# Weight gradient on one core: whole rows of G for slice 0, single transfers for slices 4 and 5, a shorter warm-up, five plain pairs at the front, and a new order of work

## The chip, the core and the metric

The kernel runs on one core of one Trainium2 chip. The metric is the device time of one execution in microseconds. Three runs of the kernel before gave 161.97, 161.98 and 162.1; their median is 161.98.

## What is computed

```python
def setup_inputs():
    batch, m, k, n = 16, 512, 1024, 768
    return {
        "input": np.random.randn(batch, m, k).astype(np.float32),
        "grad_output": np.random.randn(batch, m, n).astype(np.float32),
    }

def reference(input, grad_output):
    grad_weight = np.einsum('bmk,bmn->kn', input, grad_output)
    return grad_weight.astype(np.float32)
```

With batch and m joined, X (`input`) has 8192 rows of 1024 columns and G (`grad_output`) has 8192 rows of 768. The output is X transposed times G, 1024 x 768, a sum over the 8192 rows.

## The kernel before

**Tiling.** The rows are cut into 64 slices of 128 rows. TensorE contracts over the 128 rows of a slice: 128 columns of X are the stationary operand and 384 columns of G (its left or right half) the moving one. This document calls one such product, 128 x 128 by 128 x 384 in bf16, a *block*. The output takes 8 x 2 = 16 blocks of each slice.

**Pairs.** Slices 2u and 2u+1 form pair u. The string `LOADS` says how each of the 32 pairs is treated. An `s` pair is *plain*: 32 blocks, nothing else. A `P` pair is *merged*: it is multiplied by a scheme of the Strassen-Winograd kind, seven products of 4 blocks (q = 0 to 3), so 28 blocks, and VectorE first makes the combined operands, three steps for X (`x0`, `x1`, `x2`: lines 199, 201, 203) and three for G (`g0`, `g1`, `g2`: lines 209, 211, 213). Step `x2` writes the X block that stream B of that pair uses. Before, pairs 0 to 3 and 31 are plain and 4 to 30 are merged: 5 x 32 + 27 x 28 = 916 blocks.

**Loads.** Everything but the first transfers goes through GpSimd's DMA queue, which converts float32 to bf16 on the way (lines 170, 171, 175, 177). A pair with u >= `MERGED` comes as one transfer of G and one of X for its 256 rows (two rows for each partition). A pair with u < `MERGED` comes slice by slice. Slice 0 of G and slices 0 and 1 of X come as float32 through SyncE's and ScalarE's queues (lines 145 to 148) and are rounded to bf16 by VectorE and ScalarE (`round_by`, line 217). The kernel loads G of slice 0 in two halves of 384 columns. All other transfers stand in GpSimd's queue in the order of the pairs: G, then X.

**Warm-up.** Before the first data, line 153 runs the matmuls of `WARMUP` on constants: `("b", 512)` is a bf16 matmul of 512 columns, `("f", 512)` a float32 one, which the profile shows as two records.

**The order of the work** is written out by hand in `PLAN`, a list of tokens that is walked once; each engine executes its own part strictly in that order. The tokens:

- `C0@7.1` opens the sum of stream C, block q = 0, in PSUM bank 7 and multiplies one block; `C0.2` multiplies two more. Streams A, B, C, D are the four quarters of the output (A and B the upper half of the rows of the output, C and D the lower; A and C the left half of the columns). Streams 1, 5, 6, 7 are further products of the merged pairs. Stream A (`PACKED`) keeps its sums in banks 0 to 2 throughout.
- `c` and `v` close a sum: ScalarE copies it out (`c`, line 363), or VectorE adds it to the sum in SBUF (`v`, line 367; lines 355, 356 and 360 at the very end; line 365 when it is the first). `f` (line 295) lets ScalarE copy a sum back into a bank. `z` (line 379) puts a bank aside and `y` (line 388) adds it later on VectorE. `w` (line 395) lets GpSimd add one sum in SBUF to another.
- `x1.5`, `g0.5` are the VectorE steps of pair 5 above. `r0` to `r4` are the roundings in `ROUNDINGS`.

The last tokens before end with `... vD3 B0.2 D0.2 vB0 B3.4 vD0 B3.2 cB3`; each finished quarter block is stored at once (line 342), through SyncE's queue except the larger piece of the last one.

`SPARE_LOADS` issues the weight load once more ahead of every second matmul in a range (line 323).

Of the kernel before, what the change touches and what calls it, by code (L numbers as in the profile page):

```python
# [9 lines left out]
P = 128  # L10

LOADS = "ssssPPPPPPPPPPPPPPPPPPPPPPPPPPPs"
# [3 lines left out]
    "A0.1 A2.1 C0@7.1 A3.1 C2@6.1 cC0 r0 C3@3.1 C1@4.1 cC2 A1.1 vC3 B1@5.1 cC1 B2@7.1 D3@6.1 r1 D0@3.1 r4 r2 "  # L16
    "D1@4.1 cB1 D1.1 A0.1 B2.1 cD1 D0.1 B0@5.1 cD3 A3.1 vD0 A2.1 r3 A1.1 B3@6.1 vB0 cB2 B3.1 D3@4.1 B0@3.1 "
    "D2@7.1 vD3 D2.2 B0.1 vB3 B1@5.1 cD2 B1.1 A3.1 C3@4.1 vB1 C3.1 C2@6.2 vC3 A2.1 B3@7.1 C1@5.3 B3.1 B0.1 "
    "vC1 A1.2 C2.1 vB3 B1@4.1 D1@5.1 zcC2.20 D1.1 vB1 B2@7.2 A0.1 vB0 A0.1 A2.1 vD1 D3@6.2 D0@4.1 vB2 D0.1 "
    "A3.1 C3@5.1 vD0 D2@3.1 C0@7.2 vD3 C0.2 vD2 C0.1 C3.2 B3@6.2 vC3 B1@3.2 A3.1 vC0 D3@5.2 vB1 A1.2 B2@4.1 "  # L20
    "vD3 B2.1 D2@3.1 A0.1 yC2.20 A0.1 A3.1 D0@7.1 vB2 D0.1 A2.2 vD2 B0@5.2 D1@4.1 vD0 D1.3 vB0 C0@7.2 A3.1 "
    "vD1 A3.1 A1.1 vC0 B3.1 D2@5.3 fC1@7 B3.1 D0@4.1 vD2 D0.1 A0.2 vD0 fD3@5 C1.3 vB3 C1.1 A2.2 g0.4 cC1 "
    "C3@4.1 B2@6.1 fC2@3 B2.1 g1.4 D3.2 fB0@7 vB2 C3.1 C2.1 cD3 C2.1 g2.4 C2.1 x0.4 C2.2 A2.1 12@5.1 cC2 C3.1 "
    "x1.4 A1.2 c12 x2.4 11@6.1 C0@3.1 fC1@5 vC3 B0.3 c11 vC0 A3.1 C1.1 A0.1 B3@6.1 cC1 61@3.1 B1@4.1 vB3 cB0 "
    "B1.2 c61 73@5.1 g0.5 71@6.1 10@7.1 vB1 13@3.1 x0.5 13.1 A1.1 12@4.1 c13 10.1 A3.1 v12 71.1 c10 73.1 "
    "50@3.1 x1.5 c71 50.1 11@4.1 g1.5 51@7.1 c50 51.1 v11 60@6.1 c73 60.1 61@3.1 g0.6 c51 A2.1 53@5.1 v61 "
    "53.1 fC0@4 A0.1 63@7.1 c53 g2.5 63.1 52@3.1 g1.6 52.1 70@5.1 g2.6 70.1 c52 C0.1 x0.6 C0.1 A1.1 A3.1 cC0 "
    "72@3.1 x2.5 72.2 x1.6 70.1 73@4.1 A0.1 c70 x2.6 63.1 60.1 v73 A2.1 c63 B0@5.2 g0.7 c72 B2@4.2 c60 B2.1 "
    "vB0 62@7.1 fC1@3 62.1 g1.7 62.1 B3@6.1 vB2 B3.1 c62 C1.2 g2.7 C2@4.1 fC0@7 vB3 C2.2 f13@5 C1.1 x0.7 A2.1 "
    "A0.1 cC1 C0.1 11@6.1 vC2 11.1 f51@3 A1.1 13.1 v11 13.1 51.2 x1.7 c13 A3.1 53@6.1 cC0 x2.7 53.1 52@4.1 "  # L30
    "c51 52.1 v53 71@5.2 f50@7 C3@3.1 g0.8 C3.1 f12@6 C3.1 50.1 g1.8 50.1 12.1 g2.8 12.2 x0.8 A2.1 C3.1 c12 "
    "A1.1 A3.1 vC3 52.1 71.1 50.1 x1.8 zc52.20 73@6.2 v71 fB1@3 A0.1 61@4.2 x2.8 c50 61.1 72@5.1 v73 72.1 "
    "fB2@7 B1.2 v72 f10@6 B1.2 B2.1 v61 B2.1 cB1 63@5.1 g0.9 63.1 f51@4 10.3 fC2@3 x0.9 10.1 A1.1 cB2 A3.1 "
    "A2.1 g1.9 51.1 zc63.5 x1.9 51.1 62@7.1 c10 g2.9 62.2 x2.9 c51 A0.1 C2.1 v62 fB3@5 C2.1 60@6.2 y63.5 60.1 "
    "fB0@7 B3.2 v60 cC2 B3.1 11@4.2 y52.20 cB3 B0.2 f13@3 g0.10 B0.1 53@6.2 cB0 13.1 x0.10 13.2 f70@7 A3.1 "
    "11.1 g1.10 c13 A1.1 53.1 x1.10 70.1 f52@5 70.1 v11 70.2 A0.1 g2.10 fB2@4 52.1 x2.10 52.1 C1@3.1 c70 v53 "
    "C1.2 c52 B2.1 C3@7.1 vC1 C3.1 f72@5 B2.1 C0@6.1 vC3 C0.1 cB2 C0.1 72.1 g0.11 f73@3 B1@7.2 A2.1 c72 x0.11 "
    "A2.1 A1.1 f71@4 73.2 vC0 73.1 f63@5 71.1 g1.11 71.1 c73 71.1 x1.11 A0.1 72@6.1 c71 g2.11 72.1 63.1 x2.11 "
    "63.1 fB0@4 63.1 v72 61@3.2 c63 61.1 g0.12 B0.1 fC2@6 B0.1 60@5.1 v61 60.1 cB0 A3.1 g1.12 C2.2 v60 12@3.2 "
    "cC2 12.1 x0.12 12.1 fC3@4 B1.1 A1.1 A2.1 f53@5 g2.12 A3.1 vB1 C3.1 f51@6 C3.1 53.1 v12 53.1 cC3 50@7.2 "  # L40
    "x1.12 50.1 fC1@4 50.1 g0.13 A0.1 c53 51.2 x2.12 51.1 C1.1 g1.13 B3@5.1 c51 B3.1 v50 B3.1 f13@3 C1.1 "
    "52@6.1 vB3 52.1 cC1 13.2 x0.13 13.1 f62@4 11@5.2 c13 11.1 x1.13 A0.1 62.1 v52 62.1 f70@3 62.2 g2.13 "
    "61@7.2 c62 x2.13 70.2 v61 fC0@6 70.1 B2@4.2 v11 c70 B2.1 C0.2 vB2 f71@3 C0.1 A3.1 f73@7 10@5.1 g0.14 "
    "10.3 B1@4.1 x0.14 A2.2 zcB1.4 71.2 10.1 x1.14 f51@4 71.1 73.1 g1.14 73.1 c71 x2.14 73.1 51.1 g2.14 51.1 "
    "c73 A1.2 v10 c51 A0.1 B3@7.1 g0.15 cC0 B3.1 A3.1 63@3.1 vB3 fB1@6 63.2 B0@5.1 g1.15 f70@4 B0.1 v63 B0.1 "
    "B1.2 g2.15 72@7.2 cB1 vB0 72.1 70.1 C2@3.1 x0.15 f52@5 C2.3 53@6.2 vC2 53.1 70.1 52.1 v53 52.2 72.1 "
    "x1.15 f11@6 C1@3.2 v72 C1.1 c52 A2.1 A0.1 vC1 c70 13@7.2 60@5.1 yB1.4 f10@3 60.2 g0.16 60.1 11.2 x0.16 "
    "11.1 10.2 c11 13.1 v60 A1.2 f62@4 A3.1 x1.16 A3.1 f71@6 A2.1 v13 50@5.3 g1.16 50.1 f12@7 g0.17 62.2 "
    "zc50.18 62.1 12.1 g1.17 12.1 c62 12.1 g2.16 12.1 x2.16 71.1 fB1@4 71.1 g2.17 C3@5.1 c12 C3.1 x2.15 C3.2 "
    "x0.17 C3.1 10.1 A2.1 C0@7.1 c10 vC3 C0.2 c71 C0.1 x1.17 A3.1 A0.1 fB2@6 x2.17 A0.1 B0@3.1 g0.18 B0.2 "  # L50
    "B2.1 vC0 B2.3 vB0 B1.3 g1.18 C2@7.2 cB1 g2.18 73@5.2 cB2 vC2 73.1 C1@3.1 f61@4 C1.1 x0.18 C1.1 A1.1 "
    "zc73.3 51@6.2 vC1 51.2 C2@5.1 x1.18 fB3@3 61.2 vC2 61.3 x2.18 f53@5 63@7.2 g0.19 63.1 c61 63.1 53.2 v63 "
    "f52@4 53.1 B3.2 g1.19 f12@7 B3.1 v51 B3.1 A0.1 c53 52.1 12.1 cB3 12.1 13@5.1 x0.19 f71@6 13.2 12.1 "
    "72@3.1 x1.19 72.2 v13 72.1 71.2 v12 71.1 70@5.2 g0.20 70.1 f60@7 70.1 52.1 v72 52.2 60.1 g1.20 60.1 c52 "
    "x2.19 60.2 c71 A1.1 v70 A1.1 11@3.1 f10@6 g2.19 11.2 x0.20 11.1 fB3@5 10.3 v11 A3.2 c10 A3.1 x1.20 A2.1 "
    "fB1@3 73@4.1 x2.20 73.2 g0.21 B3.1 60.1 62@6.1 v73 62.1 c60 62.2 g2.20 B1.1 C0@4.1 g1.21 C0.1 cB1 y50.18 "
    "C0.1 C2@7.1 cB3 C2.1 g2.21 B1@3.2 v62 fB2@5 A2.3 x0.21 B2.3 vC0 C2.1 71@6.2 zcC2.1 vB1 A0.1 51@4.1 cB2 "
    "51.1 g0.22 51.1 A0.1 f72@5 50@7.1 v71 50.3 g1.22 50.1 C1@3.2 v50 C1.1 72.2 x1.21 C3@7.2 g2.22 c72 C3.1 "
    "v51 C3.2 C1.1 x0.22 A1.3 zcC1.10 12@6.1 f63@5 12.1 x1.22 12.1 53@4.1 f13@3 53.1 v12 53.2 63.1 x2.21 63.2 "
    "x2.22 63.1 B0@6.1 g0.23 B0.1 c63 B0.2 v53 B0.1 A0.1 vC3 A0.1 f70@4 13.3 f52@5 x0.23 13.1 70.2 c13 70.1 "  # L60
    "g1.23 A3.1 fC0@7 x1.23 A3.1 52.1 vB0 52.3 g2.23 61@3.2 g0.24 61.3 70.1 C0.1 v61 C0.1 c70 C0.1 62@6.1 "
    "y73.3 c52 62.2 cC0 x2.23 B3@4.3 g1.24 f71@5 B3.1 v62 A3.2 A0.1 x0.24 A0.1 A2.3 vB3 71.3 x1.24 73@4.2 "
    "yC1.10 c71 73.2 fB2@7 50@6.1 g2.24 50.1 v73 11@5.3 x2.24 B2.1 f60@4 B2.1 v11 B2.1 f62@3 B2.1 60.1 g0.25 "
# [12 lines left out]
    "C1.1 A2.2 f73@3 A1.3 vC1 fB1@6 wD2 D1.2 x2.30 73.2 cD1 x2.29 B1.2 vA3 B1.1 fB2@7 B1.2 v73 fD2@4 B1.2 "
    "C2.1 vA2 C2.1 f53@3 C2.2 vA1 C2.1 53.2 cC2 53.1 vB1 53.1 B2.1 fC3@5 B2.1 v53 B2.1 fD3@2 B2.3 f50@6 C3.1 "
    "vA0 C3.2 wB3 50.1 vB2 50.3 vC3 D2.1 fB0@7 D2.1 D3.1 v50 D3.1 cD2 B0.2 fD0@5 B0.3 fB3@3+4 vD3 B0.2 D0.2 "
    "vB0 B3.4 vD0 B3.2 cB3 "
# [8 lines left out]
MERGED = 2  # L88
# [364 lines left out]
```

## Time and profile before

| what | us |
|---|---|
| median of three runs | 161.98 |
| profiled execution, its own time | 161.87 |
| its span (first to last instruction) | 160.1 |
| outside the span | 1.77 |
| TensorE busy in the span | 154.8 |
| VectorE busy | 145.1 |
| ScalarE busy | 99.3 |
| first matmul on data | 5.04 |
| end of the last matmul | 156.7 |

TensorE is busy for 97% of the span. Between the first and the last matmul on data it stands still only in a few short places; the view of instructions in order of time shows them as an idle time in square brackets, with what ended it. The view of stages gives the busy time of each engine for a stretch of the span. In that view the columns are the stretch, its length, and for each engine the busy time with the number of instructions.

### The profile page before, as it was taken

To read this page: it belongs to the slowest core of one execution; us is meant where nothing else is said; L and a number is where in the kernel's file an instruction comes from. 1 tells how busy PE (TensorE), PEld (TensorE's weight loads), DVE (VectorE), ACT (ScalarE), POOL (GpSimd) and SP (SyncE) were. 2 spreads that over 40 slices of the span, in tenths; PEclk is the share of its full clock that TensorE was granted. 3 is DMA by queue.
4 is the path that set the end of the run, shared out by engine and by line. 5 is a ranking of instruction groups with operands and counts; after the bars stand their busy time and mean duration, and the time that the engine had idled before them with its cause. 6 is when DMAs were issued, how large, how long until landed. Compare 5 with 4: busy or idle time off the path is not lost.

```text
span 160.1 us, 2989 instructions
## 1 busy us (share of the span) xinstructions
PE 154.8 (97%) x1002; PEld 98.9 (62%) x1129; DVE 145.1 (91%) x335; ACT 99.3 (62%) x227; POOL 39.1 (24%) x73
## 2 busy tenths in 40 slices
PE   8999999999999999999999999999999999999891
PEld 3466666567677777776656566666666566666461
DVE  0579899999999999999999999999989999999991
ACT  3741028779699998985785756365465244586760
POOL 7442212222221222222122222212222100024120
PEclk9999999999999999999999999999999999999999
DMA  5999999999999999999999999999999999930696
GB/s 176 296 211 212 214 215 215 212 213 216 209 214 214 212 211 214 214 213 214 213 214 213 213 212 212 214 214 209 214 214 212 214 213 214 213 60 18 184 365 218
DMA packets 12446, 33.41 MB, mean 209 GB/s; under 512 B 1424, under 2 KB 4240, under 8 KB 12432
## 3 DMA queue, kind: packets, MB, share of 16 engines
q0 software_dynamic: 9360, 28.64, 90.4%
q1 hardware_dynamic: 2640, 3.41, 6.6%
q10 hardware_dynamic: 432, 1.18, 2.0%
q8 instruction: 8, 0.13, 0.3%
q14 instruction: 6, 0.05, 0.1%
HBM read 58.72 MB, written 3.15 MB: 386 GB/s over the span
## 4 chain that ended last, share of the span: by engine, by line
PE 78%; DMA 16%; POOL 1%; DVE 1%; issue 1%; DVEq 0%; POOLq 0%
PE bank L324 78%; DMA xp<-in_input_dram 16%; POOL gp L175 1%; DVE xp L203 1%; POOL xp L177 0%; DVE acc L365 0%; DVEq L365 0%; POOLq L437 0%
## 5 line engine op out<-in xcount | busy, mean ns | idle before, releaser
L324 PE MATMUL bank<-gp,xp 128*128 128x384 bf16 (+2 forms) x672 | 108.9, 307 | 1.1 <-DVE xp L203 0.5
L324 PEld LDWEIGHTS <-xp 128*128 128x128 bf16 x672 | 61.7, 97 | 32.4 <-DMA xp<-in_input_dram 2.0
L324 PE MATMUL bank<-ge,xe 128*128 128x384 bf16 x324 | 64.0, 326 | 0.0
L324 PEld LDWEIGHTS <-xe 128*128 128x128 bf16 x324 | 31.2, 97 | 15.3 <-DVE xe L201 0.2
L363 ACT COPY macc<-bank 128x384 f32<-128x384 f32 x63 | 28.8, 482 | 17.5 <-PE bank L324 17.3
L367 DVE TENSOR_TENSOR acc<-bank,acc 128x384 f32<-128x384 f32 x62 | 32.4, 552 | 2.8 <-PE bank L324 2.6
L295 ACT COPY bank<-macc 128x384 f32<-128x384 f32 x60 | 28.2, 485 | 6.2 <-DVE macc L367 2.8
L367 DVE TENSOR_TENSOR macc<-bank,macc 128x384 f32<-128x384 f32 x55 | 29.9, 552 | 1.1 <-PE bank L324 0.6
L295 ACT COPY bank<-acc 128x384 f32<-128x384 f32 (+2 forms) x43 | 20.1, 478 | 14.7 <-DVE acc L367 12.1
L171 POOL DMA_DIRECT2D xp<-in_input_dram x30 | 15.9, 532 | 51.9 <-DMA xp<-in_input_dram 22.8
L170 POOL DMA_DIRECT2D gp<-in_grad_output_dram x30 | 16.0, 532 | 38.3 <-PE bank L324 18.8
L363 ACT COPY acc<-bank 128x384 f32<-128x384 f32 (+1 forms) x42 | 19.4, 479 | 8.2 <-PE bank L324 7.8
L199 DVE TENSOR_TENSOR xe<-xp 128x1024 bf16<-128x1024 bf16 x27 | 18.5, 685 | 0.1
L209 DVE TENSOR_TENSOR ge<-gp 128x768 bf16<-128x768 bf16 x27 | 14.8, 550 | 0.3 <-DMA gp<-in_grad_output_dram 0.3
L203 DVE TENSOR_TENSOR xp<-xp,xe 128x512 bf16<-128x512 bf16 x27 | 11.7, 440 | 0.2
L201 DVE TENSOR_TENSOR xe<-xe,xp 128x512 bf16<-128x512 bf16 x27 | 11.3, 419 | 0.3
L379 ACT COPY aside<-bank 128x384 f32<-128x384 f32 x13 | 6.2, 479 | 8.0 <-PE bank L324 7.8
L323 PEld LDWEIGHTS <-xp 128*128 128x128 bf16 x81 | 7.9, 98 | 4.8 <-DMA xp<-in_input_dram 0.4
L395 POOL TENSOR_TENSOR acc<-acc,macc 128x384 f32<-128x384 f32 x4 | 4.2, 1061 | 22.8 <-DVE macc L360 16.5
L211 DVE TENSOR_TENSOR ge<-gp,ge 128x384 bf16<-128x384 bf16 x27 | 9.5, 352 | 0.2
L213 DVE TENSOR_TENSOR gp<-ge,gp 128x384 bf16<-128x384 bf16 x27 | 9.5, 351 | 0.1
L360 DVE TENSOR_TENSOR acc<-bank,macc 128x384 f32<-128x384 f32 (+2 forms) x14 | 6.3, 489 | 0.1
(23 smaller groups left out, 37.6 us busy)
## 6 DMA issues: line engine op xcount, KB each, us to landing
xp<-in_input_dram POOLq DMA_DIRECT2D x30, 512.0 KB, 16.9
gp<-in_grad_output_dram POOLq DMA_DIRECT2D x30, 384.0 KB, 16.7
out_dram<-acc SPq DMA_DIRECT2D x12, 192.0 KB, 2.1
xf<-in_input_dram ACTq DMA_DIRECT2D x2, 512.0 KB, 4.9
gp<-in_grad_output_dram POOLq DMA_DIRECT2D x3, 192.0 KB, 6.5
out_dram<-acc SPq DMA_DIRECT2D x6, 96.0 KB, 2.2
xp<-in_input_dram POOLq DMA_DIRECT2D x2, 256.0 KB, 7.8
gf<-in_grad_output_dram SPq DMA_DIRECT2D x2, 192.0 KB, 4.4
```

The costliest lines, as they stand in the source:

```text
L170: nc.gpsimd.dma_start(out=gp, in_=G[rows, :].rearrange("(p m) n -> p m n", m=2))
L171: nc.gpsimd.dma_start(out=xp, in_=X[rows, :].rearrange("(p m) k -> p m k", m=2))
L199: nc.vector.tensor_sub(out=xe[:, 0:2, :], in0=x[:, 1::-1, :], in1=x[:, 3::-2, :])
L201: nc.vector.tensor_sub(out=xe[:, 2, :], in0=xe[:, 0, :], in1=x[:, 0, :])
L203: nc.vector.tensor_add(out=x[:, 1, :], in0=x[:, 2, :], in1=xe[:, 2, :])
L209: nc.vector.tensor_add(out=ge[:, 0:2, :], in0=g[:, 0:2, :], in1=g[:, 1::2, :])
L211: nc.vector.tensor_add(out=ge[:, 2, :], in0=g[:, 3, :], in1=ge[:, 0, :])
L213: nc.vector.tensor_add(out=g[:, 1, :], in0=ge[:, 2, :], in1=g[:, 2, :])
L295: nc.scalar.copy(out=tile_[:, t0 : t0 + c1 - c0], in_=sum_of(p, q)[:, c0:c1])
L324: nc.tensor.matmul(tile_[:, t0 : t0 + c1 - c0], stat, mov[:, c0:c1], start=start, stop=True, skip_group_check=True,)
L363: nc.scalar.copy(out=d, in_=b)
L367: nc.vector.tensor_add(out=d, in0=b, in1=d)
```

## The change

Six edits:

- `LOADS` has five plain pairs at the front instead of four, so pairs 0 to 4 and 31 are plain and 5 to 30 merged: 6 x 32 + 26 x 28 = 920 blocks.
- `MERGED` goes from 2 to 3: slices 4 and 5 (pair 2) come slice by slice.
- G of slice 0 comes as one transfer of whole rows.
- The second float32 warm-up matmul has 384 columns instead of 512.
- The first seven roundings are put into `PLAN` as `r10` to `r16`, and so get an order of their own.
- `PLAN` is a new order throughout; `SPARE_LOADS` ends at 440 instead of 455.

```diff
-LOADS = "ssssPPPPPPPPPPPPPPPPPPPPPPPPPPPs"
+LOADS = "sssssPPPPPPPPPPPPPPPPPPPPPPPPPPs"
...
-    "A0.1 A2.1 C0@7.1 A3.1 C2@6.1 cC0 r0 C3@3.1 C1@4.1 cC2 A1.1 vC3 B1@5.1 cC1 B2@7.1 D3@6.1 r1 D0@3.1 r4 r2 "
-    "D1@4.1 cB1 D1.1 A0.1 B2.1 cD1 D0.1 B0@5.1 cD3 A3.1 vD0 A2.1 r3 A1.1 B3@6.1 vB0 cB2 B3.1 D3@4.1 B0@3.1 "
...
-    "C1.1 A2.2 f73@3 A1.3 vC1 fB1@6 wD2 D1.2 x2.30 73.2 cD1 x2.29 B1.2 vA3 B1.1 fB2@7 B1.2 v73 fD2@4 B1.2 "
-    "C2.1 vA2 C2.1 f53@3 C2.2 vA1 C2.1 53.2 cC2 53.1 vB1 53.1 B2.1 fC3@5 B2.1 v53 B2.1 fD3@2 B2.3 f50@6 C3.1 "
-    "vA0 C3.2 wB3 50.1 vB2 50.3 vC3 D2.1 fB0@7 D2.1 D3.1 v50 D3.1 cD2 B0.2 fD0@5 B0.3 fB3@3+4 vD3 B0.2 D0.2 "
-    "vB0 B3.4 vD0 B3.2 cB3 "
+    "r11 r10 r15 r13 r0 C1@6.1 r16 r12 r14 B2@4.1 cC1 D0@3.1 C3@5.1 vB2 A3.1 A0.1 cC3 C2@7.1 vD0 B0@4.1 "
+    "D1@6.1 A2.1 r3 r2 A1.1 r1 B1@3.1 r4 B1.1 C2.1 cD1 D3@5.2 B0.1 B3@6.1 cD3 B3.1 vB0 A1.1 A2.1 cB3 C0@5.1 "
...
+    "c12 A3.1 x1.30 10@7.2 v11 f61@4 10.1 13@6.1 A1.1 g2.30 A1.1 f60@3 v13 61.3 v10 60.1 f71@6 60.2 v61 60.1 "
+    "f62@7 C0.1 71.1 x2.30 A0.1 f63@4 62.1 v60 62.3 v71 f73@3 63.1 A3.2 v63 f72@6 A0.1 wC1 A0.1 A2.1 v62 A2.1 "
+    "A1.2 vA3 f70@7 72.3 vA1 f53@4 72.1 70.2 v72 70.2 73.1 vA2 f50@6 73.3 vA0 53.3 v73 53.1 fC1@0 53.1 50.1 "
+    "v70 f52@1 50.1 wC3 50.2 v53 fD3@3 C1.2 fD0@7 C1.2 C0.1 v50 C0.1 f51@4 wB3 D3.2 D0.1 fD2@2 D0.1 52.1 vC0 "
+    "cC1 52.2 fC2@6 51.1 vD3 51.3 vD0 C2.1 fC3@3 C2.2 v51 fD1@5 C2.1 C3.2 fB1@7 C3.2 vC2 D2.2 cC3 B1.1 v52 "
+    "B1.1 fB0@0 B1.3 B0.2 vB1 B0.1 fB3@3+1 B0.2 vD2 B0.1 fB2@4 B0.2 D1.2 vB0 B2.3 vD1 B2.2 B3.2 vB2 B3.3 cB3 "
...
-WARMUP = [("b", 512), ("f", 512), ("f", 512), ("b", 512)]
+WARMUP = [("b", 512), ("f", 512), ("f", 384), ("b", 512)]
...
-MERGED = 2
+MERGED = 3
...
-SPARE_LOADS = range(200, 455)
+SPARE_LOADS = range(200, 440)
...
-    nc.sync.dma_start(out=gf[:, LEFT], in_=G[0:P, LEFT])
+    nc.sync.dma_start(out=gf, in_=G[0:P, :])
     nc.scalar.dma_start(out=xf[0], in_=X[0:P, :])
-    nc.sync.dma_start(out=gf[:, RIGHT], in_=G[0:P, RIGHT])
     nc.scalar.dma_start(out=xf[1], in_=X[P : 2 * P, :])
...
-    round_by("DVE", g0, gf, 0, 192)
-    round_by("ACT", g0, gf, 192, NH)
-    round_by("DVE", x0, xf[0], 0, P)
-    round_by("ACT", x0, xf[0], 2 * P, 4 * P)
-    round_by("DVE", x0, xf[0], P, 2 * P)
-    round_by("DVE", x0, xf[0], 4 * P, 6 * P)
-    round_by("ACT", x0, xf[0], 6 * P, 8 * P)
-    ROUNDINGS = [
-        ("DVE", g0, gf, NH, N),
-        ("DVE", x1, xf[1], 4 * P, 6 * P),
-        ("DVE", x1, xf[1], 0, 2 * P),
-        ("ACT", x1, xf[1], 6 * P, 8 * P),
-        ("ACT", x1, xf[1], 2 * P, 4 * P),
-    ]
+    ROUNDINGS = {
+        0: ("DVE", g0, gf, NH, N),
+        1: ("DVE", x1, xf[1], 4 * P, 6 * P),
+        2: ("DVE", x1, xf[1], 0, 2 * P),
+        3: ("ACT", x1, xf[1], 6 * P, 8 * P),
+        4: ("ACT", x1, xf[1], 2 * P, 4 * P),
+        10: ("DVE", g0, gf, 0, 192),
+        11: ("ACT", g0, gf, 192, NH),
+        12: ("DVE", x0, xf[0], 0, P),
+        13: ("ACT", x0, xf[0], 2 * P, 4 * P),
+        14: ("DVE", x0, xf[0], P, 2 * P),
+        15: ("DVE", x0, xf[0], 4 * P, 6 * P),
+        16: ("ACT", x0, xf[0], 6 * P, 8 * P),
+    }
```

## The prediction

> **What bounds the kernel now.** I read the page's busy shares first, then the chain of waits in order of time.
>
> ```profile
> PE 154.8 (97%) x1002; PEld 98.9 (62%) x1129; DVE 145.1 (91%) x335; ACT 99.3 (62%) x227; POOL 39.1 (24%) x73
> ...
> 3.50 8.41 DMA xp<-in_input_dram
> ...
> 12.20 17.80 DMA xp<-in_input_dram
> 30.00 0.05 issue
> 30.05 117.88 PE bank L324 x776
> 147.93 1.24 DVE xp L203 x2
> 149.17 0.05 issue
> 149.22 7.51 PE bank L324 x51
> ```
>
> Columns of the chain: start, length, what. Until 30.0 us the end is set by X arriving, from then by TensorE, but for one place near 148 us where VectorE's step `x2` (line 203) is late. Next, TensorE's instructions in order of time; square brackets are idle time.
>
> ```profile
> 4.57 0.58 PE L153 MATMUL bank<-const-bfloat16-1.0 128*128 128x512 bf16 x1
> 5.04 1.49 PE L324 MATMUL bank<-gp,xp 128*128 128x384 bf16 x10
> 6.78 9.28 PE L324 MATMUL bank<-gp,xp 128*128 128x384 bf16 x62 [0.25 <-DVE gp L217]
> 16.23 12.22 PE L324 MATMUL bank<-gp,xp 128*128 128x384 bf16 x84 [0.17 <-DMA xp<-in_input_dram]
> ...
> 30.05 0.99 PE L324 MATMUL bank<-gp,xp 128*128 128x384 bf16 x6 [0.26 <-DMA xp<-in_input_dram]
> ```
>
> Within a row, full blocks start 0.162 us apart; starts are what count, as the ends are modelled. Measured in starts, TensorE loses 0.41 at 6.3 (right half of G of slice 0), 0.34 at 15.7, 0.42 at 29.5 and 0.12 at 34.1 (X), and 0.62 at 148.4: 1.9 in all. Five stops of 0.04 to 0.06 and the split blocks of stream A add about 0.4 more. The last stop, all engines in order of time:
>
> ```profile
> 147.54 1.00 POOL L395 TENSOR_TENSOR acc<-acc,macc 128x384 f32<-128x384 f32 x1 [1.54 <-DVE macc L356]
> ...
> 147.84 1.31 DVE L203 TENSOR_TENSOR xp<-xp,xe 128x512 bf16<-128x512 bf16 x2
> ...
> 149.22 0.99 PE L324 MATMUL bank<-gp,xp 128*128 128x384 bf16 x5 [0.45 <-DVE xp L203]
> ```
>
> The first `x2` lasts 0.98 beside GpSimd's merge `w` (line 395), against a median of 0.42 over the 27 of line 203, and B's blocks wait for the second one.
>
> Last, the stages (start:end and length, then busy us and instructions of each engine):
>
> ```profile
> 40.00:60.00 20.00, 20.00 (x133) 14.48 (x197) 19.69 (x48) 18.05 (x43) 4.77 (x9) 1.00 1.07 213
> 60.00:80.00 20.00, 20.00 (x135) 14.18 (x180) 19.61 (x47) 15.66 (x36) 4.77 (x9) 1.00 1.07 214
> 80.00:100.00 20.00, 20.00 (x132) 12.32 (x131) 19.66 (x48) 13.52 (x31) 5.06 (x10) 1.00 1.07 212
> 100.00:120.00 20.00, 20.00 (x136) 12.49 (x133) 18.63 (x45) 10.75 (x25) 5.01 (x10) 1.00 1.07 213
> ```
>
> TensorE is full and VectorE (third figure) nearly so, with 0.3 to 1.4 of 20 free.
>
> **One plain pair more, and the early stops.** Four blocks more (920 against 916) cost 4 x 0.162 = +0.65, if TensorE has something to do all the time. At the front it has not, so I count blocks against arrivals. Walking `PLAN` before, block 172 is the first of pair 6 and stands at 34.43; X of pair 6 lands at 34.31 (the idle weight load there ends at 34.35). In the new `PLAN` the first block of pair 6 is number 176. Both have 744 blocks left from there. The next pairs agree: the first blocks of pairs 7, 8, 9 are 198, 224, 251 before and 202, 228, 255 after, and before they start at 38.71, 43.03 and 47.49, each 0.08 to 0.24 behind its X (38.63, 42.94, 47.25). So the front is paced by arrivals through pair 9, and the four extra blocks fill the time that TensorE spent standing at 29.5 and 34.1. Extra blocks and removed stops cancel: **0 net**. If TensorE were not held by arrivals, the four blocks would show as +0.65.
>
> **The front itself.** G of slice 0 as one transfer removes the wait at 6.3. But the new order takes its first block of slice 1 as number 12 (before: 13, at 7.59), and that needs G of slice 1, which lands at 7.51 as the first transfer of GpSimd's queue. So block 12 stands near 7.6 all the same, and from there 164 blocks x 0.1626 put block 176 at 34.26, ahead of X of pair 6. The start has slack twice over: 12 blocks from 5.04 would reach only 6.99. The first block may therefore come 0.5 later for nothing; its rounding of 256 columns lasts 0.286 against 0.23 for the 128 columns before. The new order of roundings costs nothing under the same cover. With half of G gone from SyncE's queue, one issue of 0.42 there is saved, with nothing behind it until the stores.
>
> **Slices 4 and 5 one by one.** Two GpSimd issues more (0.55 each) on an engine with 24% busy: 0. The pieces are half as long. GpSimd's queue moved 208 GB/s from 8 to 11 us, where slices came one by one, and 213 from 12 to 20, where pairs came whole. A pair is 0.917 MB in bf16: 4.41 against 4.31, so everything behind comes 0.10 later: **+0.10**, paid in full, as the front is paced by arrivals. Bounds: 0, and +0.3 if the two issues in front of the rest cost their landing order something too. What it buys, slice 4 at its X (about 14.2) instead of at 16.19, removes the stop at 15.7, which is inside the count above.
>
> [...]
>
> **Shorter warm-up.** Two records of 0.853 become two of 0.640: it ends 0.43 sooner, at about 4.5. The first block waits for rounding, not for the warm-up, so 0 on the path, unless the clock minds (rival).
>
> **Fewer spare loads** (120 for 128): TensorE is 20.00 of 20 with 197 loads in a stage as with 131, so 0.
>
> **The middle.** Over the 600 blocks from the 760th to the 160th before the end the list has, before, 79 `v`, 9 `y`, 66 `x`, 70 `g`; after, 78, 12, 68, 68. At 0.465 a start for `v` and `y` and 0.27 to 0.61 for the steps that is +0.9 for VectorE. In the four stages above plus 120 to 140 (9.90 and 9.59 of 10) it has 2.9 free of 100, so it is hidden; if not, +0.9 (rival). Fewer fills and copies (91 and 90 against 102 and 105) relieve ScalarE, which sets nothing.
>
> **The end.** The new list has `x2.30` 87 blocks before the end (before: 50, with `x2.29` at 48 and B's blocks at 45 and 44), B's blocks of pairs 29 and 30 at 24 and 23, and the three `w` at 78, 54 and 46, all behind the last `x` step. No step with two SBUF operands is left on VectorE beside a `w`. The stop of 0.62 goes: **-0.62**. Bounds: 0 if another wait takes its place, -0.62. The last five blocks and the store of the last piece are as before, so the 3.4 us behind the last matmul stay.
>
> **Sum**, against the profiled execution: 161.87 + 0 + 0.10 - 0.62 = 161.35. That execution lies 0.11 under the median of the runs, so on the median's scale 161.46; I take **161.45**.
>
> **Rivals.**
>
> 1. *A new wait of the same size* (a bank not yet emptied, a step of VectorE just late): for it, VectorE has under 3% free and every sum is queued strictly; against it, the list before got through 600 blocks with five stops of 0.06. About +0.5: 161.95.
> 2. *VectorE becomes the bound in the middle.* It decides if less than 0.9 of its 2.9 free can be used, since its free moments are waits for a matmul's end. Against it: 15 direct follow-ups of dependent steps (`x0` then `x1` and so on) after, 24 before. 161.45 + 0.9 = 162.35.
> 3. *The clock opens later.* In the warm-up the first 512 bf16 columns took 0.38 to the next start, while 0.162 for 384 means 0.216 for 512: TensorE begins 1.76 times slower. Now it stands still 0.4 longer before data. If that kept it slow for as long again as the whole warm-up (0.78 to 4.8, 4.0 us), until 9.0, blocks would take 0.286 from 5.1 on: 13.6 by 9.0, so block 176 at 35.4 instead of 34.53: +0.9, 162.35. The page's clock row shows full speed from the first slice and decides nothing. For it: the stop falls just before the data. Against: only 0.4 of over 4 us is idle. [...]
> 4. *Transfers come sooner.* GpSimd's queue delivers nothing until the first halves are in; whole rows could start it 0.3 earlier. All arrivals and block 12 move with it: 161.15.
>
> **Chances.** Forecast 0.50, rival 1 0.16, rival 2 0.12, rival 3 0.12, rival 4 0.10. The forecast's own range is 161.2 to 161.75 (0 to +0.3 for the transfers, and up to 0.15 fewer won at the end). To hold 8 in 10 I go from 161.05 (under rival 4) to 162.3 (rival 1 whole, the near halves of 2 and 3). A measurement here tells 0.2% from no change, 0.32 us, so faster is below 161.66. Faster: 0.45 of the forecast and rival 4, 0.55; same: the rest of the forecast and rival 1, 0.21; slower: rivals 2 and 3, 0.24.
>
> **What would show it.** TensorE's blocks start 0.162 apart from the first on (else rival 3). Block 12 stands near 7.6, and the first blocks of pairs 6 and 9 near 34.5 and 47.6. All `x2` last 0.42, and no idle time of TensorE over 0.1 stands in the last 20 us. VectorE's free time from 40 to 140 falls to about 2, with no TensorE stop put down to it. I am wrong if the first block of pair 9 stands later than 48.0, or if the stops behind it sum to over 0.6.

## The result, and the profile after

The changed kernel took 162.58 us, the median of 12 runs, against 161.95 for the kernel before in runs beside it. The ratio is 1.0051, with a 95% interval of 1.0034 to 1.0069: slower, by some 0.6 us. The forecast was 161.45. The 12 runs fall into two groups: seven from 162.18 to 162.59, and five from 163.07 to 163.57. The profiled execution belongs to the first group: its own time is 162.48, with a span of 160.7 (before: 161.87 and 160.1).

The page of the changed kernel, first the busy shares, then the chain of waits in order of time (start, length, what):

```profile
PE 154.7 (96%) x1007; PEld 99.8 (62%) x1127; DVE 142.3 (89%) x330; ACT 88.6 (55%) x200; POOL 38.7 (24%) x74
```

```profile
2.45 7.35 DMA xp<-in_input_dram
9.80 0.28 issue
10.08 11.96 DMA xp<-in_input_dram
22.04 0.05 issue
22.09 135.27 PE bank L320 x896
```

The chain hangs on X transfers until 22.04, where it was 30.00 before, and then runs on TensorE alone to the last matmul; the step `x2` near 148 us is gone from it. The view of TensorE's instructions in order of time, start of the changed kernel (start, length, what, idle time before it):

```profile
4.14 0.63 PE L149 MATMUL bank<-const-bfloat16-1.0 128*128 128x512 bf16 x1
5.97 15.47 PE L320 MATMUL bank<-gp,xp 128*128 128x384 bf16 x105 [1.20 <-ACT xp L213]
22.09 2.12 PE L320 MATMUL bank<-gp,xp 128*128 128x384 bf16 x12 [0.65 <-DMA xp<-in_input_dram]
```

The stops at 6.3, 15.7, 29.5 and 34.1 have become one, ahead of 22.09. It is 0.82 long in starts, and the block behind it is the first that needs X of pair 3 (block 93 of the new list; its counterpart before, block 91, stood at 20.64 with no wait). The first block on data comes at 5.97 against 5.04. The end of the changed kernel in the same view:

```profile
148.64 1.79 PE L320 MATMUL bank<-gp,xp 128*128 128x384 bf16 x10
150.26 1.30 PE L320 MATMUL bank<-ge,xe 128*128 128x384 bf16 x7
151.40 5.94 PE L320 MATMUL bank<-gp,xp 128*128 128x384 bf16 x40
```

No row here carries an idle time: the stop of 0.62 has gone. All 26 `x2` steps now last what they should, in the view of line 199 (durations in ns as least/median/most, then first and last start):

```profile
L199 DVE TENSOR_TENSOR xp<-xp,xe x26: 410/416/426, 36.5 to 143.0; 128x512 bf16<-128x512 bf16 x26
```

A comparison of block starts tells where the time went. Blocks are counted from 0 in the order of the list, as in the prediction, and the last row is the first matmul of the last block, which is split:

| | before | after, forecast | after, measured |
|---|---|---|---|
| first block on data | 5.04 | up to 0.5 later, for nothing | 5.97 |
| block 12 | (13: 7.59) | near 7.6 | 8.02 |
| first block of pair 3 | 20.64 | - | 22.09 |
| first block of pair 6 | 34.43 | 34.53 | 35.61 |
| first block of pair 9 | 47.49 | near 47.6 | 48.68 |
| last block | 156.33 | - | 156.90 |

From pair 9 to the last block both kernels have 665 blocks left: 108.84 before, 108.22 after (to the start of the very last matmul 109.01 and 108.44). The difference, 0.57 to 0.62, is what the forecast took from the end. So the miss lies ahead of pair 6: 35.61 against 34.53 is +1.08, and the profiled execution's own time is 1.13 above the 161.35 of the sum. Behind 22.09 TensorE no longer waits for arrivals: X of pairs 6 and 9 is in at 34.64 and 47.68, 0.97 and 1.00 ahead of its first block. So nothing behind takes the delay up. Two questions follow: why X of pair 3 came so late, and what the five runs above 163 are.

### The profile page after: what moved, and what is told of

It reads as the page before. It is cut to its first block, busy times and chain, and to the rows that moved or that the text cites. A ratio compares the mean times of both kernels' runs of the same rounds, so it can differ in the third digit from the quotient of the medians.

```text
span 160.7 us, 2958 instructions
## 1 busy us (share of the span) xinstructions
PE 154.7 (96%) x1007; PEld 99.8 (62%) x1127; DVE 142.3 (89%) x330; ACT 88.6 (55%) x200; POOL 38.7 (24%) x74
## 3 DMA queue, kind: packets, MB, share of 16 engines
q10 hardware_dynamic: 432, 1.18, 1.9%
## 4 chain that ended last, share of the span: by engine, by line
PE 84%; DMA 12%; POOL 1%; issue 1%; DVE 0%; DVEq 0%; POOLq 0%
PE bank L320 84%; DMA xp<-in_input_dram 12%; POOL gp L171 1%; DVE acc L361 0%; DVEq L361 0%; POOLq L433 0%
## 5 line engine op out<-in xcount | busy, mean ns | idle before, releaser
L320 PEld LDWEIGHTS <-xp 128*128 128x128 bf16 x689 | 64.5, 98 | 34.4 <-DVE xp L213 2.3
L320 PE MATMUL bank<-ge,xe 128*128 128x384 bf16 x312 | 61.4, 326 | 0.0
L359 ACT COPY macc<-bank 128x384 f32<-128x384 f32 x66 | 30.7, 481 | 21.8 <-PE bank L320 21.4
L363 DVE TENSOR_TENSOR acc<-bank,acc 128x384 f32<-128x384 f32 x67 | 35.6, 551 | 5.8 <-PE bank L320 5.0
L320 PEld LDWEIGHTS <-xe 128*128 128x128 bf16 x312 | 30.1, 97 | 13.7
L291 ACT COPY bank<-macc 128x384 f32<-128x384 f32 x64 | 30.2, 484 | 10.8 <-DVE macc L363 7.0
L363 DVE TENSOR_TENSOR macc<-bank,macc 128x384 f32<-128x384 f32 x48 | 26.0, 550 | 1.5 <-PE bank L320 0.9
L291 ACT COPY bank<-acc 128x384 f32<-128x384 f32 (+2 forms) x28 | 12.9, 473 | 20.5 <-DVE acc L363 19.4
L359 ACT COPY acc<-bank 128x384 f32<-128x384 f32 (+1 forms) x24 | 11.4, 474 | 10.9 <-PE bank L320 10.6
L319 PEld LDWEIGHTS <-xp 128*128 128x128 bf16 x70 | 6.8, 98 | 4.2
L391 POOL TENSOR_TENSOR acc<-acc,macc 128x384 f32<-128x384 f32 x3 | 2.9, 997 | 20.9 <-DVE macc L356 20.9
L319 PEld LDWEIGHTS <-xe 128*128 128x128 bf16 x50 | 4.9, 98 | 2.9 <-DVE xe L195 0.2
```

The lines of the kernel that those rows point to most:

```text
L291: nc.scalar.copy(out=tile_[:, t0 : t0 + c1 - c0], in_=sum_of(p, q)[:, c0:c1])
L319: nc.tensor.ldweights(stat)
L320: nc.tensor.matmul(tile_[:, t0 : t0 + c1 - c0], stat, mov[:, c0:c1], start=start, stop=True, skip_group_check=True,)
L359: nc.scalar.copy(out=d, in_=b)
L363: nc.vector.tensor_add(out=d, in0=b, in1=d)
```

## The experiments

Two theories for the profiled execution. *F (code fetch)*: X of pair 3 is late because a transfer of the queue `instruction` falls into it, a fetch of code by its name; that the code is TensorE's is the author's reading. The view of DMA queues (queue, kind: packets, MB, share of 16 engines) for 19.9 to 20.9 of the changed kernel:

```profile
q0 software_dynamic: 76, 0.20, 101.1%
q8 instruction: 1, 0.02, 5.6%
```

and for 21.0 to 22.4 of the kernel before:

```profile
q0 software_dynamic: 100, 0.30, 109.4%
q8 instruction: 1, 0.02, 4.2%
```

One packet of 16 KB, and 5.6% of 16 engines over 1.0 us is 0.90 us of one DMA engine (before, 4.2% over 1.4: 0.94). It starts at 19.96 after, and at 21.36 before. Each load of GpSimd's queue leaves 16 completions in the trace. Of those of X of pair 3, 15 came between 20.34 and 20.73 after, and the sixteenth at 22.04. Before, that X was in by 20.54, and it was G of pair 4 that came as 15 by 22.36 and one at 23.48, where TensorE did not stop. That the late sixteenth is a part that shares a DMA engine with the fetch is inferred from these times; the views do not name the engine. *S (start)*: the whole rows of G come later than the halves, all roundings with them, and everything behind is late for that. For the five long runs there is rival 3 of the prediction, the clock that opens later.

**G of slice 0 in halves again, in the new order.**

```diff
-    nc.sync.dma_start(out=gf, in_=G[0:P, :])
+    nc.sync.dma_start(out=gf[:, LEFT], in_=G[0:P, LEFT])
...
+    nc.sync.dma_start(out=gf[:, RIGHT], in_=G[0:P, RIGHT])
```

> The changed kernel with G of slice 0 loaded in two halves again, nothing else touched. Theory F (a 16 KB transfer on the queue named instruction, 0.9 us on one of the 16 DMA engines, starts at 19.96 in the changed kernel and holds up X of pair 3, which lands at 22.04 instead of some 20.8; TensorE's block 93 waits for it until 22.09): the first block comes back from 5.97 to about 5.1, block 93 still waits for X of pair 3 until 21.7 to 22.1, and the time stays at 162.2 to 162.6. Theory S (the late start of 0.9 us is what the change costs): the time falls by 0.5 or more, to 162.0 or below. If the runs near 163.4 come from the long standstill between warm-up and data, they disappear here too.

163.72 (ratio 1.0083, 1.0053 to 1.0112), from four runs of 161.96 to 162.47 and eight of 163.65 to 165.44. TensorE's start in order of time:

```profile
5.28 0.34 PE L321 MATMUL bank<-gp,xp 128*128 128x384 bf16 x1 [0.51 <-DVE xp L214]
6.90 5.37 PE L321 MATMUL bank<-gp,xp 128*128 128x384 bf16 x37 [1.29 <-DVE gp L214]
```

The new order asks for the right half with its second block, so the halves bring a new stop, block 12 stands at 8.69, and the start is no test of S. The fetch began at 20.57 here, X of pair 3 landed at 20.66, and the first block of pair 3 ran at 21.94 without a wait: a start late enough hides the fetch. The long runs became more, with a second standstill after the warm-up.

**The wait for pair 3 four instructions earlier** (one block of stream A, which is split into two matmuls with a weight load each, moved behind it).

```diff
-D3@4.2 A2.1 C3@7.1 vD3 C3.3 vB1 C3.1 C1@3.2
+D3@4.2 C3@7.1 vD3 C3.3 vB1 C3.1 A2.1 C1@3.2
```

> The changed kernel with one token of the list moved: A2.1 (one block in two pieces, four TensorE instructions, slice 5) from just ahead of C3@7.1 to just behind C3.1, so that TensorE's first instruction on pair 3 stands four instructions earlier, where it stands in the kernel before. [...] Theory S: no change, 162.4 to 162.7.

163.22 (1.0066, 1.0042 to 1.0089), six runs: two of 162.41 and 162.43, four from 163.05 to 163.67. The profiled one is of the first two. The fetch began at 19.72 and X of pair 3 landed at 21.81, the second as far behind the first as without the edit. So a wait that stands earlier did not put the fetch off: it began 0.24 before the 19.96 of the changed kernel.

**Four weight loads more at the front of the kernel before.**

```diff
-if begun_matmuls[0] in SPARE_LOADS and begun_matmuls[0] % 2:
+if begun_matmuls[0] in (*range(21, 28), *SPARE_LOADS) and begun_matmuls[0] % 2:
```

> The kernel before with four weight loads issued twice (at matmuls 21, 23, 25 and 27), nothing else. Theory F: the wait for X of pair 3 stands four instructions later in TensorE's stream, as in the changed kernel; the queue instruction's transfer starts before X of pair 3 has landed, X of pair 3 lands near 21.8 instead of 20.54, TensorE stops there for about 1.1 us, and the time rises by 0.4 to 0.9, to 162.4 to 162.9. Theory S: four loads that lie beside matmuls cost nothing, 161.95 as before.

161.94 (1.0004, 0.999 to 1.0018); fetch at 21.15, X of pair 3 at 20.63. The rise of 0.4 to 0.9 that F forecast did not come: four instructions move the fetch by 0.2, too little to reach the transfer. The edit was too small to decide between the theories.

**Twenty-four weight loads more in the kernel before, once ahead of pair 3 and once behind it.** The load is repeated, so nothing else changes.

```diff
-if begun_matmuls[0] in SPARE_LOADS and begun_matmuls[0] % 2:
+if begun_matmuls[0] in (*range(21, 69), *SPARE_LOADS) and begun_matmuls[0] % 2:
```

> The kernel before with 24 weight loads issued twice between matmuls 21 and 67. They lie beside matmuls and take no TensorE time. Theory F: TensorE asks for its next 16 KB of code at a given count of instructions, so some 12 blocks or 2 us sooner: the transfer of queue instruction starts at 19.2 to 19.6 instead of 21.36, X of pair 3 lands at 21.6 to 21.9 instead of 20.54, block 91 stands near 21.8 instead of 20.64, and the time rises by 0.3 to 0.9, to 162.3 to 162.9. Theory S: 161.95 as before.

The control:

```diff
-if begun_matmuls[0] in SPARE_LOADS and begun_matmuls[0] % 2:
+if begun_matmuls[0] in (*range(131, 179), *SPARE_LOADS) and begun_matmuls[0] % 2:
```

> Control for the run before it: the same 24 second loads between matmuls 131 and 177, behind the first transfer of queue instruction. Theory F: that transfer stays at 21.1 to 21.4, X of pair 3 lands at 20.5 to 20.7, and the time stays at 161.85 to 162.1. If extra loads cost time by themselves, it rises as in the run before it.

Early: 162.30 (1.0024, 1.0015 to 1.0033). Late: 161.98 (1.0005, 0.9996 to 1.0014). TensorE in order of time, early loads:

```profile
21.35 2.94 PE L324 MATMUL bank<-gp,xp 128*128 128x384 bf16 x18 [0.54 <-DMA xp<-in_input_dram]
```

and late loads:

```profile
14.78 13.84 PE L324 MATMUL bank<-gp,xp 128*128 128x384 bf16 x94
```

With the loads early, the fetch begins at 18.92 in place of 21.36, X of pair 3 lands at 21.30 in place of 20.54, and TensorE waits for it, in a kernel that has none of the change's edits. Pair 3 then starts 0.71 late (21.35 against 20.64), and 0.37 of that reaches the median; the stop of 0.42 that the kernel before has at 29.5 is gone here and takes up most of the rest. With the same number of loads behind pair 3, the fetch stays at 21.54, X lands at 20.61, and TensorE runs through from 14.78. The stop follows the count of instructions ahead of the fetch, not the added work: this is F, shown in one direction.

**Twenty-four TensorE instructions fewer in the changed kernel, with the long warm-up.** Twelve early blocks of stream A, which are split into two matmuls, run as one. This kernel leaves the split out without giving the sums their proper columns, so these twelve sums land in the wrong columns of their banks and part of its output is wrong: it serves to measure time, not to be used.

```diff
-WARMUP = [("b", 512), ("f", 512), ("f", 384), ("b", 512)]
+WARMUP = [("b", 512), ("f", 512), ("f", 512), ("b", 512)]
...
+        joined = p == "A" and len(parts) == 2 and done[p, q] < 6
...
+            if joined:
+                if i == 0:
+                    continue
+                t0, c0, c1 = 0, 0, NH
```

> The changed kernel with the second warm-up matmul at 512 columns, and the first six slices of stream A, q = 1 and 2, as one matmul of 384 columns each instead of one of 128 and one of 256 columns: the same columns in 24 TensorE instructions fewer. The sums of these twelve blocks land in the wrong columns of their banks, so that part of the output is left wrong; the time of every engine is otherwise as with 512 columns of warm-up (162.49). Theory F: TensorE asks for its next 16 KB of code 12 blocks later, the transfer of queue instruction starts at 20.9 to 21.9 instead of 19.89, X of pair 3 lands at 20.6 to 20.9, TensorE does not wait ahead of block 93, which stands at 21.0 to 21.2 instead of 21.95, and the time falls by 0.5 to 0.9, to 161.6 to 162.0. Theory S: 162.4 to 162.6.

161.67 (0.9983, 0.9975 to 0.9992). The number of columns multiplied is the same. TensorE in order of time:

```profile
14.75 15.45 PE L325 MATMUL bank<-gp,xp 128*128 128x384 bf16 x100
```

The fetch begins at 22.17, X of pair 3 lands at 20.68, and its first block runs at 21.25 with no stop. Against the changed kernel with the long warm-up alone (next) this is 0.82 less, the length of the stop. F is shown in the other direction as well, with the size of the loss.

**The long warm-up in the changed kernel, otherwise as it is.**

```diff
-WARMUP = [("b", 512), ("f", 512), ("f", 384), ("b", 512)]
+WARMUP = [("b", 512), ("f", 512), ("f", 512), ("b", 512)]
```

> The changed kernel with the second float32 warm-up matmul back at 512 columns. Theory C (five of the changed kernel's twelve runs took 163.07 to 163.57 because the clock sometimes opens late, TensorE being idle for 1.4 us before data): the runs near 163.4 become rarer or disappear and the median falls to 162.3 to 162.5. Theories F and S: the warm-up is off the path, the median stays within 162.4 to 162.7 with runs near 163.4 as before.

162.49 (1.0028, 1.0017 to 1.0039), six runs from 162.37 to 162.55: none above 163. The fetch stays at 19.89, X of pair 3 at 21.90. So the warm-up does not make X late. That it has to do with the five long runs does not rest on these six alone. Of the changed kernel and its variants, none of 28 runs with the long warm-up lies above 163 (this kernel, the one with 24 instructions fewer, and the left half first, below), and 18 of 33 with the shorter one do (the changed kernel, with the halves, with the earlier wait, and the three executions below).

**The warm-up shorter still** (the second float32 matmul left out).

```diff
-WARMUP = [("b", 512), ("f", 512), ("f", 384), ("b", 512)]
+WARMUP = [("b", 512), ("f", 512), ("b", 512)]
```

> The changed kernel with the second float32 warm-up matmul left out, so that TensorE stands idle from about 3.3 to 6.0 us before data. Theory C: the clock opens late in nearly every run, the profile shows blocks 0.32 apart for some microseconds behind 6.0, block 93 stands at 22.8 or later, and most runs take 163.0 to 164.5. Rival (the warm-up is not what makes the changed kernel's slow executions): 162.2 to 162.6 with a few near 163.4, as the changed kernel.

163.09 (1.008, 1.0055 to 1.0106), six runs from 162.65 to 164.36. TensorE's weight loads in order of time (each row of x1 is one block):

```profile
7.81 0.15 PEld L320 LDWEIGHTS <-xp 128*128 128x128 bf16 x1 [0.17 <-issue]
8.13 0.15 PEld L320 LDWEIGHTS <-xp 128*128 128x128 bf16 x1 [0.17 <-issue]
8.45 3.58 PEld L320 LDWEIGHTS <-xp 128*128 128x128 bf16 x26 [0.17 <-issue]
```

The blocks stand 0.32 apart until 8.45, and 0.162 from there: TensorE runs at half its rate after the start. So the mechanism of rival 3 occurs.

**The changed kernel itself, three more profiled executions**, to have a long run with its trace.

> The changed kernel again, one profile. Theory C: if the time is near 163.4, the first blocks stand 0.32 apart until the clock opens at 8 us or later, and block 93 stands at 22.6 or later; if it is near 162.5, blocks stand 0.162 apart from 6.2 on at the latest. Rival: a slow execution shows the usual rate at the front and loses its time elsewhere.

163.24, 162.56 and 162.54. The first is a long run. Its weight loads:

```profile
5.80 0.14 PEld L320 LDWEIGHTS <-xp 128*128 128x128 bf16 x2 [2.14 <-DVE xp L213]
6.10 0.15 PEld L320 LDWEIGHTS <-xp 128*128 128x128 bf16 x1 [0.16 <-issue]
...
8.34 0.15 PEld L320 LDWEIGHTS <-xp 128*128 128x128 bf16 x1 [0.17 <-issue]
8.66 3.32 PEld L320 LDWEIGHTS <-xp 128*128 128x128 bf16 x22 [0.17 <-issue]
```

and those of the profiled execution above, which is one of the short ones:

```profile
5.97 6.07 PEld L320 LDWEIGHTS <-xp 128*128 128x128 bf16 x44 [2.31 <-DVE xp L213]
```

In the long run the spacing is 0.32 up to about 9.5, in the short one 0.162 from the first block. By stages (stretch, length, then busy us and instructions of TensorE, its weight loads, VectorE, ScalarE, GpSimd, then granted clock, DMA share, GB/s) the long run

```profile
6.00:8.00 2.00, 2.00 (x7) 0.91 (x6) 1.62 (x7) 1.26 (x5) 0.18 (x1) 1.00 1.14 216
8.00:10.00 2.00, 2.00 (x11) 1.24 (x10) 0.09 (x1) 0.87 (x3) 0.88 (x2) 1.00 1.14 209
```

does 18 matmuls in 4 us, the short run

```profile
6.00:8.00 2.00, 2.00 (x14) 1.28 (x15) 1.86 (x7) 1.82 (x6) 0.12 (x1) 1.00 1.16 232
8.00:10.00 2.00, 2.00 (x17) 1.31 (x15) 0.98 (x4) 1.34 (x4) 0.94 (x2) 1.00 1.12 207
```

31. The column of the granted clock says 1.00 in all four and decides nothing; the spacing does. The trace's record of the full clock begins at 9.56 in the long run, where the spacing changes, and at 5.43, 5.31 and 4.75 in the three short ones, ahead of their first block. That one long run was traced; that the other long runs are of the same kind is inferred from their times. Being slow has a second effect: the fetch is reached later (21.45), X of pair 3 is in at 20.66, and the 0.82 is not paid. The first block of pair 3 stands at 22.85, 0.70 behind that of the next execution (22.15), and the times differ by 0.68.

**The shorter warm-up alone, in the kernel before.**

```diff
-WARMUP = [("b", 512), ("f", 512), ("f", 512), ("b", 512)]
+WARMUP = [("b", 512), ("f", 512), ("f", 384), ("b", 512)]
```

> The kernel before with the second float32 warm-up matmul at 384 columns, nothing else. Its first block stands at 5.04, so TensorE is idle for 0.5 before data instead of 0.1. Theory C, with the length of the standstill deciding: all runs at 161.8 to 162.2, or at most one or two above 162.6. If the shorter warm-up alone decides, four or more of the runs lie above 162.6.

161.93 (0.9997, 0.9988 to 1.0006), eleven runs, the longest 162.16. By itself it loses nothing. From the start of the last warm-up matmul to the first block it has 4.15 to 5.21, 1.06; the changed kernel has 1.66 to 1.83 in its four profiled executions, as whole rows of G make the first block late at the same time. The changed kernel with the long warm-up has 1.24, and no long run in six. A late clock is not confined to the changed kernel, though. In the profiled execution of the kernel before with 24 late loads, 0.64 after the last warm-up matmul, the weight loads are:

```profile
5.21 0.77 PEld L324 LDWEIGHTS <-xp 128*128 128x128 bf16 x5 [1.34 <-DVE xp L217]
6.15 0.15 PEld L324 LDWEIGHTS <-xp 128*128 128x128 bf16 x1 [0.17 <-issue]
6.47 0.15 PEld L324 LDWEIGHTS <-xp 128*128 128x128 bf16 x1 [0.17 <-issue]
6.79 1.28 PEld L324 LDWEIGHTS <-xp 128*128 128x128 bf16 x9 [0.17 <-issue]
```

Here too blocks stand 0.32 apart, but only until 6.79, where the record of the full clock begins. Of this kernel's eleven runs none is longer than 162.26.

**Whole rows of G alone, in the kernel before.**

```diff
-    nc.sync.dma_start(out=gf[:, LEFT], in_=G[0:P, LEFT])
+    nc.sync.dma_start(out=gf, in_=G[0:P, :])
...
-    nc.sync.dma_start(out=gf[:, RIGHT], in_=G[0:P, RIGHT])
```

> The kernel before with G of slice 0 in one transfer of whole rows, nothing else. Theory S (the late start is a loss of its own): the first block comes at 5.6 to 6.0 instead of 5.04, block 13 moves from 7.59 to 7.9 or later, and the time rises by 0.3 or more, to 162.25 or above. Rival (the front is paced by arrivals, as the prediction had it): the first block is late but block 13 and the block at 34.4 move by less than 0.15, and the time stays at 161.8 to 162.1.

162.00 (1.0005, 0.9996 to 1.0014). The first block moves from 5.04 to 5.53, block 13 from 7.59 to 7.75 (0.16, just over the 0.15 that the rival allowed), and the first block of pair 6 is at 34.41 (34.43). A start that is half a microsecond late is taken up by the stops behind it, as the forecast said.

**The left half first, its blocks ahead of the others, and the long warm-up**: an attempt to keep the change and mend its start. Of the three edits only the order of the list is shown; G in halves and the long warm-up are as above.

```diff
-    "r11 r10 r15 r13 r0 C1@6.1 r16 r12 r14 B2@4.1 cC1 D0@3.1 C3@5.1 vB2 A3.1 A0.1 cC3 C2@7.1 vD0 B0@4.1 "
-    "D1@6.1 A2.1 r3 r2 A1.1 r1 B1@3.1 r4 B1.1 C2.1
+    "r11 r10 r15 r13 C1@6.1 r16 r12 r14 C3@5.1 cC1 A3.1 A0.1 cC3 C2@7.1 A2.1 A1.1 r0 B2@4.1 D0@3.1 vB2 vD0 B0@4.1 "
+    "D1@6.1 r3 r2 r1 B1@3.1 r4 B1.1 C2.1
```

> The changed kernel with its start mended three ways: G of slice 0 in two halves, the first seven blocks all from the left half (C1 C3 A3 A0 C2 A2 A1, then B2 D0 B0 D1 B1), the second float32 warm-up matmul at 512 columns. Theory S (the late start is what remains of the loss): first block near 5.1, block 12 near 7.7 instead of 7.85 to 8.0, and the time falls with the start to 162.2 or below. Theory F (X of pair 3 is late because of the 16 KB transfer of queue instruction): that transfer starts between 19.4 and 19.9, X of pair 3 lands near 21.8, block 93 stands at 21.9 whatever the start, and the time stays at 162.3 to 162.5. Theory C (the clock opens late in some runs when TensorE stands idle between warm-up and data): all runs within 0.4 of each other, none near 163.4.

162.30 (1.0018, 1.0008 to 1.0027), eleven runs up to 162.57. The first block is at 5.28, but a new stop on a bank that VectorE has yet to empty puts block 12 at 8.18, the fetch begins at 20.00, X of pair 3 lands at 22.05, and its first block runs at 22.10. The gain at the start is lost to the fetch, as F said.

**The end, in the kernel before: `x2` ahead of a sum.**

```diff
-vC0 fD1@7 A0.1 C1.2 v52 fC2@5
+vC0 fD1@7 A0.1 C1.2 x2.30 x2.29 v52 fC2@5
...
-wD2 D1.2 x2.30 73.2 cD1 x2.29 B1.2
+wD2 D1.2 73.2 cD1 B1.2
```

> The kernel before with two tokens of its list moved: x2.30 and x2.29 from behind wD2 to just ahead of v52, so that VectorE makes them before GpSimd's merge wD2 can begin. Theory P (the stop of 0.62 at 148.4 came from VectorE's step x2, lengthened to 0.98 beside GpSimd's merge, and from its late place): both x2 last 0.42, the stop is gone, the time falls by 0.4 to 0.6, to 161.4 to 161.6. Rival: VectorE is full in the last 15 us, the wait only moves to the eviction that now comes later (v52), and the time stays at 161.8 to 162.0.

162.55 (1.0038, 1.0026 to 1.0051). Both `x2` last 0.42, but the stop stays:

```profile
148.98 2.11 PE L324 MATMUL bank<-gp,xp 128*128 128x384 bf16 x12 [0.43 <-ACT bank L295]
```

It now waits for a fill from a sum that `v52` closes, and that comes later. Arrivals are 0.33 later as well, and the stores at the end take 2.5 to 2.6 to land instead of 1.9 to 2.0; why was not found.

**The end, in the kernel before: no merge on GpSimd beside `x2`.** `wD2` is left out, and VectorE adds that sum at the end.

```diff
-vC1 fB1@6 wD2 D1.2 x2.30
+vC1 fB1@6 D1.2 x2.30
...
-v50 D3.1 cD2 B0.2
+v50 D3.1 vD2 B0.2
```

> The kernel before without GpSimd's merge wD2: block D2 is closed at the end by VectorE (vD2) instead of ScalarE (cD2), which adds the shared sum in the same step, 0.47 more on VectorE near the end. Theory P (GpSimd's merge beside VectorE's step x2 makes the stop at 148.4): both x2 last 0.42, the stop falls from 0.62 to under 0.15, and the time falls by 0.3 to 0.5, to 161.4 to 161.7. Rival (VectorE is full there and any step more or less only moves the stop): 161.8 to 162.1.

161.75 (0.9988, 0.9979 to 0.9996): faster than the kernel before and than the changed one. TensorE at that place:

```profile
147.78 0.49 PE L324 MATMUL bank<-ge,xe 128*128 128x384 bf16 x2
148.11 2.17 PE L324 MATMUL bank<-gp,xp 128*128 128x384 bf16 x12
```

The stop of 0.62 is 0.05, and the last block starts at 155.76 instead of 156.33. Both `x2` last 0.42 here. So the `x2` of 0.98 beside GpSimd's merge was the cause of the stop, shown. Only 0.2 of the 0.57 reaches the median: the addition now lies behind the last matmuls, and the last stores land in 2.3 in place of 1.9 to 2.0.

## Why the prediction was wrong, step by step

**The step that failed: "So the front is paced by arrivals through pair 9", with arrivals moved by +0.10 alone.** Up to pair 3 TensorE does wait for arrivals, but the arrivals are not the load queue's alone: with a fetch begun between 18.92 and 20.00 X of pair 3 landed at 21.30 to 22.05 (five profiled executions), with one begun at 20.57 or later at 20.54 to 20.68 (six). And behind that wait the changed kernel is paced by TensorE itself (X of pair 6 lands 0.97 ahead of its first block), so no later stop takes the loss up. In the forecast the first block of pair 6 stood 0.10 behind its place before. It stood 1.18 behind. Of the 1.08 between the two, 0.82 is the wait for X of pair 3 behind the fetch (shown: early loads make the wait in the kernel before, and fewer instructions take 0.82 off the changed one). The 0.26 left is what remains of the late start, by sum and not by a run of its own: block 12 was put near 7.6 by the landing of G of slice 1 (7.60, as forecast), but stood at 8.02, since twelve blocks from 5.97 reach only 7.92. The forecast let the first block come 0.5 late; it came 0.93 late, as the whole of G and X of slice 0 are loaded at the same time and both land late (5.28 and 5.50; before 4.40 for the left half and 4.73). With the fetch out of the way (24 instructions fewer, long warm-up) the kernel takes 161.67, 0.22 above the forecast, close to that 0.26.

The page of before lists the fetches as two "instruction" queues (packets, MB, share of 16 engines), and the prediction passed over them:

```profile
q8 instruction: 8, 0.13, 0.3%
q14 instruction: 6, 0.05, 0.1%
```

An average over the span hides what one such transfer of 0.9 us went with: of the 16 completions of X of pair 3, 15 were in by 20.73, the last came at 22.04, and TensorE waited for it until 22.09. The forecast walked the list in blocks and never in instructions.

**Shorter warm-up, "0 on the path, unless the clock minds".** It minds, by the times in 5 of 12 runs, together with the later first block. So rival 3 came true in part of the runs, and in the one long run that was traced by its own mechanism: blocks 0.32 apart until about 9.5, for which it had 0.286 until 9.0. The price is near its 0.9 (the medians of the two groups are 163.37 and 162.48), but made up otherwise: in the traced long run block 13 stands 1.57 later (9.76 against 8.19), and the 0.82 of the fetch is not paid. In the median it is worth some 0.1 (162.58 against 162.49 with the long warm-up), which is within the noise.

**Sum.** 161.45 + 0.82 (fetch) + 0.26 (start) is 162.53, and the 162.58 leaves 0.05, in which the long runs' pull on the median lies. The 0.26 is taken from one profile, so that the sum comes out this well is in part luck.

**What held.** One plain pair more shows no loss of 0.65: without the fetch the kernel with 920 blocks takes 161.67, and that with 916 161.95, less the 0.62 that the end gave, is 161.33; the late start covers most of the 0.34 between. The end gave 0.57 to 0.62, the forecast size, and for the forecast reason. VectorE is no bound (rival 2): by stages it has 2.66 of 100 free from 40 to 140, where about 2 was said, and no stop of TensorE there. From pair 9 to the end no new wait of the size of rival 1 stands. Single transfers for slices 4 and 5 removed the stop at 15.7. Their +0.10 can be read in the landings: from X of slice 3 to the last of X of slice 5 it is 4.28 before (11.91 to 16.19) and 4.41 after (12.01 to 16.42), 0.13 more. Transfers did not come sooner (rival 4).

**What stays open.** Which instruction sets the fetch off, and so why the new order puts it 1.4 us sooner: in the changed kernel and its variants it began with 201 to 211 matmuls and weight loads started, in the kernel before and its variants with 219 to 229, and edits of four instructions shifted it by some 0.2. How much of the front's late start is the order of roundings and how much the whole rows. Why the stores of two variants landed later. One of eleven runs of the kernel with four loads more took 163.2, and its cause is not known.

## What to carry to other kernels

Where a front is paced by loads, walk the new order in instructions as well as in blocks: here 24 weight loads more put a fetch of 16 KB 2.44 us sooner (18.92 against 21.36) and X of pair 3 0.76 later (21.30 against 20.54). Look at a load's last completion and not at the queue's mean rate: in the changed kernel the last of 16 came 1.31 behind the fifteenth, while over the whole span the queue `instruction` (q8) shows 0.3% of 16 engines. Try a start with a longer warm-up too, and judge it by several runs: of the changed kernel and its variants 18 of 33 with the shorter one lay above 163 and none of 28 with the longer one, so that a single run can miss the difference. Look for an operation that lasts far longer than its median: the `x2` of 0.98 against 0.42 led to the stop of 0.62, which fell to 0.05 without the merge beside it.

## What the runs showed of the hardware

**Code fetch.** In the profiled executions of before and after the queue `instruction` (q8) ran eight transfers of 16 KB, 15.2 to 20.1 us apart, with 220 to 279 matmuls and weight loads begun from one to the next; 15 of the 16 were 0.89 to 1.02 us long, one 1.27. No view says whose code they carry. What the runs show is that the first one moves with the count of TensorE's instructions: 24 weight loads more ahead of it put it at 18.92 instead of 21.36, 24 behind it left it at 21.54, and 24 instructions fewer put it at 22.17 instead of 19.89. From the load into which it fell, the last of 16 completions came 0.87 to 1.31 behind the other 15 (before: G of pair 4, at 23.48; after: X of pair 3, at 22.04), until after the next fetch, one of 8 KB at 32.35 (before: 26.86), a second completion fell back. Later in the span more did, and the last of a load stayed 1.3 to 1.9 behind the first to the end of the loads (0.4 to 0.6 ahead of the first fetch), in both kernels. TensorE did not stop beside the first fetch in the kernel before, and lost 0.82 us in the changed one.

**Clock.** After a warm-up of over 3 us (from 0.78 to the start of its last matmul at 4.14 to 4.57), 1.66 us from that start to the first block left TensorE with blocks 0.32 apart, about twice the usual 0.162, until 9.5 in one execution, while 1.83 did not in another, and 0.64 left it there until 6.79 in a third. So the length of the standstill does not decide alone. The record of the full clock begins at 8.55 and 9.56 in the two executions with blocks 0.32 apart past 8 us (2.73 and 1.66 of standstill), and between 4.2 and 6.8 in all others; these records are all 153.60 or 157.01 us long. Why one start loses the full rate and another with as long a standstill does not was not shown.
